# A two-layer GLA/FoX trunk on one core: key decay and output gate on GpSimd, a table root in two tasks, other modulation rates, more fills among the first sums, and the forget-gate product behind its weight tile

## The chip, the core and the metric

The kernel runs on one core of a Trainium2 chip. The engines it uses are TensorE (PE for its matmuls, PEld for its weight loads), VectorE (DVE), ScalarE (ACT), GpSimd (POOL) and SyncE (SP), which issues the DMAs. Each works through its own instructions in order, and they wait for one another by semaphores. The metric is the device time of one execution in microseconds, as the median of several. A change of less than 0.2% of it, 4.8 us, can't be told from none.

## The reference

A trunk of two layers on 256 tokens of width 2048, in fp32. Each layer is a token mixer and a gated MLP, and each of these is normalised, modulated by a conditioning vector `c`, and added back through a modulated gate:

```python
for i in range(2):
    sh_m, sc_m, g_m, sh_f, sc_f, g_f = split(c @ w_mod[i] + b_mod[i])
    h = rmsnorm(x, norm_mix[i]) * (1 + sc_m) + sh_m
    x = x + (1 + g_m) * mixer[i](h)            # 0: GLA, 1: FoX
    h = rmsnorm(x, norm_ffn[i]) * (1 + sc_f) + sh_f
    x = x + (1 + g_f) * conv_ffn(h)
```

The GLA mixer is a chunked gated linear attention with four heads. The change touches three places of it:

```python
q, k, v, r, a = split(h @ w_in)
b = cumsum(log_sigmoid(a @ w_gate + b_gate) / 16)       # in chunks of 64 tokens
k_inv = k * exp(-b);   k_end = k * exp(b_last - b)      # the key decay
o = attention(q * exp(b), k_inv, k_end, v)
o = rmsnorm(o, g_norm) * silu(r)                        # the root, the output gate
return o @ w_out
```

The FoX mixer is a causal softmax attention with a forget gate of 16 columns, `fl`, which come out of the same input product as q, k, v and the output gate: `q, k, v, og, fl = split(h @ w_in)`.

## The kernel before

Every weight matrix is streamed from HBM in tiles of 128 x 1024 fp32, loaded by SP into a ring of eight buffers (`RING`). A tile is split in two: ACT casts it to the reduced format of the matmul (`wh`, L140), and DVE subtracts that from the original (`wl`, L144). The activations are split in the same way, and three products are summed for each pair: high by high, high by low, low by high. So a weight tile costs PE 24 matmuls of 128x256 (L779, `stream_a`) or 12 of 128x512 (L860, `stream_b`). There are four buffers for split tiles, so ACT and DVE split up to three tiles ahead of the one PE works on (`AHEAD`).

`next_w` hands out the next tile and, on the way, issues the loads and splits of those ahead. Around every tile `tick()` runs other work: steps of the adaLN modulation, and tasks of a list `side`, both at a rate per tile held in `pace`. The order in which the program is written is then rearranged engine by engine by a scheduler, within what `tc.issue_after(x)` allows: what is written under it isn't placed ahead of instruction x.

**Modulations.** `c @ w_mod` is not done on PE: each 128-row piece of `w_mod` is multiplied by its element of c and added up on DVE (L289, L291, `acc`), 1.28 us for 128x1024, one piece in a step. When a sum is complete it rests for `REST` tiles, and is then turned by PE transposes (L322), added along the free axis on ACT (L326), and finished on DVE (L335, L344, L347). `BG0` and `BG1` are the rates of these steps in two stages of GLA, `N1` is the number of tiles over which the remaining steps are spread in the product behind GLA, and `LATE` the credit that this stage begins with.

**The start.** The first modulation, the shift of the first layer, is needed before anything else, and is computed on PE: pieces of `w_mod` by columns of c (L1517), a row copy on ACT (L1523), and eight one-column matmuls (L1526). Between these sums stand "fills" (L1563): matmuls on a constant that only keep PE busy, `KEEP` of them behind each sum. The first layer's normalised input `h` comes in blocks of 4, 5 and 7 tiles, since its modulation arrives in pieces, and the GLA input product runs over q, k, v0, v1, r0, r1 and a once for each block.

**GLA.** In the third block (`gla_rest`) the side tasks make the gate's cumulative sums, then the decayed queries (L1056 to L1062) and keys (`decay_k`, L1073 and L1074), the scores of the four heads (PE L1103, ACT L1108, DVE L1109 and L1110, mask on POOL L1112), their application to v (`apply`, PE L1125 and L1127, ACT L1131 and L1134), the sums of squares (DVE L1137 and L1138, PE L1141, DVE L1142 into `pvar`), their root (`table_root`: POOL L532, an ACT table function L533, and four refining operations on POOL, L534 to L537, into `grs`), the normalisation (`normalise`, with a broadcast by PE L445 and DVE L1153), and the output gate (`open_gate`: Silu on ACT L1168, product on DVE L1170). The result is split for the output product (ACT L682, DVE L683), which is `add_residual` with key `g_m`.

**FoX.** The v part of the input product runs over 16 row blocks in `stream_b`. From block 9 on (`GATE_AT`) `gate_part` adds the forget gate's product: it fetches a narrow weight tile of 128x368 (split into `nw`) and multiplies it with all h blocks so far, three matmuls of 128x256 each (L1231), then three more at each following block.

Of the kernel before, what the change touches and what calls it, by code (L numbers as in the profile page):

```python
# [18 lines left out]
P = 128  # L19
# [25 lines left out]
KEEP = 3  # L45
# [9 lines left out]
GP0 = 0.9  # L55
# [7 lines left out]
BG0, BG1 = 1.1, 1.1  # L63
N1, N2, N3, N4 = 22, 151, 150, 154
LATE = -3.0
# [15 lines left out]
def kernel(  # L81
# [184 lines left out]
    def mod_tasks(l, key, f0=0, fn=D, wide=False, defer=False, turn=False):  # L266
# [8 lines left out]
        def chunk(c0, kt, st):  # L275
# [5 lines left out]
            def f():  # L281
# [13 lines left out]
                elif last:  # L295
# [8 lines left out]
                    resting.append([REST, finish])  # L304
# [224 lines left out]
    def table_root(q, src, scale):  # L529
# [3 lines left out]
        nc.scalar.activation(q, v, AF.Abs_reciprocal_sqrt)  # L533
        nc.gpsimd.tensor_tensor(out=t, in0=v, in1=q, op=ALU.mult)  # L534
        nc.gpsimd.tensor_tensor(out=t, in0=t, in1=q, op=ALU.mult)
        nc.gpsimd.tensor_scalar(out=t, in0=t, scalar1=-0.5, scalar2=1.5, op0=ALU.mult, op1=ALU.add)
        nc.gpsimd.tensor_tensor(out=q, in0=t, in1=q, op=ALU.mult)  # L537
# [309 lines left out]
    def stream_b(kts, c0, lhs, base=None, extra=None):  # L847
# [4 lines left out]
        def mms(tt, k, wh, wl, lh, ll, n_=None):  # L852
            first, last = base is None and k == kts[0], k == kts[-1]
            ts_ = slice(tt * P, (tt + 1) * P)
            for hf in range(2):
                hs_ = slice(hf * 512, (hf + 1) * 512)
                o = ps[tt * 2 + hf]
                for i, (l_, w_) in enumerate(((lh, wh), (ll, wh), (lh, wl))):
                    if n_ is None or n_ == i:
                        mm = nc.tensor.matmul(o, l_[:, ts_], w_[:, hs_], start=first and i == 0, stop=last and i == 2,  # L860
                                              skip_group_check=True)
            return mm.ins
# [126 lines left out]
    def gla_rest(l, kts, pieces, piece, fold, parts):  # L989
# [80 lines left out]
        def decay_k(f0):  # L1070
            def f():
                fs = slice(f0, f0 + 4)
                nc.vector.tensor_tensor(out=kend[:, fs, :], in0=kinv[:, fs, :192], in1=ee[:, fs, :], op=ALU.mult)  # L1073
                nc.vector.tensor_tensor(out=kinv[:, fs, :], in0=kinv[:, fs, :], in1=enb[:, fs, :], op=ALU.mult)  # L1074
# [69 lines left out]

        def scale_of(hd):
            return lambda: table_root(grs[:, 2 * hd:2 * hd + 4], pvar[:, 2 * hd:2 * hd + 4], 1.0 / 512.0)
# [15 lines left out]
        side.extend((apply(2), apply(3), normalise(0), normalise(1), scale_of(2)))  # L1162
        pace["side"], pace["sacc"] = GP0, 0.0
        def open_gate(g, b):
            def f():
# [4 lines left out]
                nc.vector.tensor_tensor(out=o, in0=o, in1=th, op=ALU.mult)  # L1170
# [18 lines left out]
    def fox(l, h):  # L1189
# [32 lines left out]
        def gate_part(k):  # L1222
# [4 lines left out]
            for kk in range(0 if k == GATE_AT else k, k + 1):  # L1227
                gh, gl = h(kk)
                cs = slice(kk * FH, kk * FH + P)
                for i, (w_, r_) in enumerate(((gates["w"][0], gh), (gates["w"][0], gl), (gates["w"][1], gh))):  # L1230
                    nc.tensor.matmul(gates["p"][:, :T], w_[:, cs], r_, start=(kk == 0 and i == 0),  # L1231
                                     stop=(kk == KT - 1 and i == 2), skip_group_check=True)

# [287 lines left out]
    def early_finish(key, f0):  # L1521
# [3 lines left out]
        for m in range(HEAD):  # L1525
            nc.tensor.matmul(pt[:, m:m + 1], rows_[:, m * P:(m + 1) * P], one, start=(m == 0), stop=(m == HEAD - 1),  # L1526
                             skip_group_check=True)
# [22 lines left out]
    for i, args in enumerate(todo):  # L1550
# [8 lines left out]
        elif args[0] == "sh_m":  # L1559
            pw = psA.tile([P, 512], F32, tag="a", name=nm("pw"))  # L1560
            with tc.issue_after(summed):
                for _ in range(KEEP):
# [106 lines left out]
```

## Time and profile before

| | |
|---|---|
| median of 3 runs | 2410.9 us (2410.68 to 2413.03) |
| the profiled execution | 2411.13 us, of which the span is 2409.4 us |
| PE, PEld | busy 98% and 94% of the span |
| DVE, ACT, POOL | 78%, 56%, 2% |
| the chain that ended last | PE 92%, DVE 3%, DMA 3%, ACT 1%, issue 1% |
| HBM | 633 MB read, 264 GB/s over the span |

The profile is of one execution. A group of instructions has a line, an engine, an operation and names as `out<-in`; then come its count, its busy time, the mean of one, and the idle time of the engine just before its instructions, with what ended that idle time. In a timeline a row gives the start, the duration of a run of like instructions, and in brackets the idle time ahead of it. Matmuls overlap, so how far apart two of them start says more than their durations. PEclk is the share of full speed that TensorE was granted.

### The profile page before, as it was taken

The page shows a single profiled execution, that of the slowest core. Times are in us where ns is not written, and L with a number is a line of the kernel's source. Part 1 is how long each engine was busy: PE and PEld are TensorE (multiplying, and loading weights), DVE is VectorE, ACT ScalarE, POOL GpSimd, SP SyncE. Part 2 cuts the span into 40 slices and gives each one's busy share as a digit, 9 for nine tenths or more (in the row PEclk, how much of TensorE's full clock was granted, in tenths as well). Part 3 has the DMA queues.
Part 4 walks back from the last instruction along what each step waited for, and adds up shares of the span by engine and source line. Part 5 has one row for each costly group of instructions (what it writes and reads, how often), then busy time and mean ns, then how long its engine had stood idle before and what let it go on. Part 6 is the DMA issues. An engine that isn't in the chain of part 4 may idle for free.

```text
span 2409.4 us, 46946 instructions
## 1 busy us (share of the span) xinstructions
PE 2369.6 (98%) x19028; PEld 2274.7 (94%) x19030; DVE 1886.2 (78%) x2478; ACT 1347.1 (56%) x1932; POOL 45.6 (2%) x93
## 2 busy tenths in 40 slices
PE   7999999999999999999999999999999999999998
PEld 5899889999999999999888879999999999999998
DVE  5787979887679999986678888888777777777544
ACT  4668764645776566443554455545755555565433
POOL 0000000000000000000000201100000000000000
PEclk9999999999999999999999999999999999999999
DMA  9898869797669988998589877786777777766552
GB/s 375 326 353 297 312 229 325 275 361 273 199 200 310 314 310 311 324 315 301 158 297 314 303 267 236 241 296 234 227 236 237 228 235 236 235 206 216 192 191 101
DMA packets 188293, 638.31 MB, mean 265 GB/s; under 512 B 23849, under 2 KB 24859, under 8 KB 187692
## 3 DMA queue, kind: packets, MB, share of 16 engines
q1 hardware_dynamic: 187112, 634.12, 77.0%
q8 instruction: 149, 2.44, 0.4%
q10 hardware_dynamic: 964, 1.20, 0.1%
q14 instruction: 68, 0.56, 0.1%
HBM read 633.14 MB, written 2.10 MB: 264 GB/s over the span
## 4 chain that ended last, share of the span: by engine, by line
PE 92%; DVE 3%; DMA 3%; ACT 1%; issue 1%; DVEq 0%; SPq 0%; ACTq 0%
PE pa L779 74%; PE pa L860 14%; DMA wm<-in_w_mod_dram 1%; DVE wl L144 1%; DMA w<-in_fox_w_in_dram 0%; DVE acc L291 0%; DMA w<-in_gla_w_in_dram 0%; DVE hn L623 0%; PE pm L1103 0%; PE pm L1330 0%; PE pm L1276 0%; PE pm L1294 0%; ACT wh L140 0%; PE pm L1293 0%; PE pm L1125 0%
## 5 line engine op out<-in xcount | busy, mean ns | idle before, releaser
L140 ACT CAST wh<-w 128x1024 fp32r<-128x1024 f32 x816 | 852.1, 1049 | 903.2 <-PE pa L779 651.4
L144 DVE TENSOR_TENSOR wl<-w,wh 128x1024 fp32r<-128x1024 f32 x816 | 991.7, 1218 | 405.4 <-ACT wh L140 399.3
L779 PE MATMUL pa<-h,wh 128*128 128x256 f32 x7168 | 1223.5, 278 | 5.0 <-DVE h L653 3.6
L779 PEld LDWEIGHTS pa<-h,wh 128*128 128x128 f32 x7168 | 1073.9, 188 | 10.5 <-DVE h L653 4.2
L779 PE MATMUL pa<-h,wl 128*128 128x256 f32 x3584 | 966.3, 277 | 1.9 <-DVE wl L144 1.9
L779 PEld LDWEIGHTS pa<-h,wl 128*128 128x128 f32 x3584 | 662.5, 188 | 2.7 <-DVE wl L144 2.5
L779 PE MATMUL pa<-op,wh 128*128 128x256 f32 x3840 | 651.6, 277 | 0.4 <-DVE op L683 0.2
L779 PEld LDWEIGHTS pa<-op,wh 128*128 128x128 f32 x3840 | 573.0, 188 | 1.4 <-DVE xT L912 1.0
L779 PE MATMUL pa<-op,wl 128*128 128x256 f32 x1920 | 518.0, 276 | 0.0
L291 DVE SCALAR_TENSOR_TENSOR acc<-wm,cT,acc 128x1024 f32<-128x1024 f32 (+2 forms) x360 | 444.4, 1235 | 15.1 <-DMA wm<-in_w_mod_dram 13.9
L779 PEld LDWEIGHTS pa<-op,wl 128*128 128x128 f32 x1920 | 355.0, 188 | 0.0
L860 PE MATMUL pa<-wh,h 128*128 128x512 f32 x1024 | 312.0, 394 | 0.2 <-ACT h L644 0.2
L860 PEld LDWEIGHTS pa<-wh,h 128*128 128x128 f32 x1024 | 191.1, 188 | 40.3 <-ACT h L644 0.9
L860 PE MATMUL pa<-wl,h 128*128 128x512 f32 x512 | 191.8, 394 | 0.0
L860 PEld LDWEIGHTS pa<-wl,h 128*128 128x128 f32 x512 | 96.5, 189 | 19.5
L1382 ACT ACTIVATE y<-u,cw 128x256 f32<-128x256 f32 x176 | 101.7, 599 | 3.3 <-DVE act L1398 1.3
L1385 DVE SCALAR_TENSOR_TENSOR y<-u,cw,y 128x254 f32<-128x254 f32 x176 | 83.3, 479 | 2.9
L1383 DVE SCALAR_TENSOR_TENSOR y<-u,cw,y 128x255 f32<-128x255 f32 x176 | 84.0, 477 | 0.0
L1404 ACT COPY u<-pa 128x512 f32<-128x512 f32 x112 | 63.6, 582 | 2.1 <-PE pa L779 1.2
L644 ACT ACTIVATE h<-hn,mod 128x256 fp32r<-128x256 f32 x58 | 32.4, 596 | 14.0 <-DVE hn L623 11.3
L1392 ACT ACTIVATE u<-y 128x256 f32<-128x256 f32 x88 | 36.0, 413 | 3.3 <-DVE y L1385 3.1
L1398 DVE TENSOR_TENSOR act<-u,y 128x256 f32<-128x256 f32 x88 | 36.7, 420 | 1.4
(274 smaller groups left out, 1044.5 us busy)
## 6 DMA issues: line engine op xcount, KB each, us to landing
wm<-in_w_mod_dram SPq DMA_DIRECT2D x320, 512.0 KB, 5.3
w<-in_ffn_w_up_dram SPq DMA_DIRECT2D x320, 512.0 KB, 4.5
w<-in_ffn_w_down_dram SPq DMA_DIRECT2D x176, 512.0 KB, 4.6
w<-in_fox_w_in_dram SPq DMA_DIRECT2D x128, 512.0 KB, 5.2
w<-in_gla_w_in_dram SPq DMA_DIRECT2D x96, 512.0 KB, 7.1
w<-in_gla_w_out_dram SPq DMA_DIRECT2D x32, 512.0 KB, 5.9
w<-in_ffn_w_up_dram SPq DMA_DIRECT2D x64, 256.0 KB, 4.0
w<-in_fox_w_out_dram SPq DMA_DIRECT2D x32, 512.0 KB, 5.1
```

Of the source, the lines that this page charges most:

```text
L140: order["b"], order["c"] = order["c"], nc.scalar.copy(out=hi, in_=src).ins
L144: order["v"] = nc.vector.tensor_tensor(out=lo, in0=src, in1=hi.bitcast(F32), op=ALU.subtract).ins
L291: nc.vector.scalar_tensor_tensor(out=st["a"], in0=wt[:, j, :], scalar=col, in1=st["a"], op0=ALU.mult, op1=ALU.add)
L644: hot = nc.scalar.activation(hi, t, AF.Identity, scale=sc, bias=sh).ins
L779: mm = nc.tensor.matmul(o, w_[:, ms], r_, start=(first and i == 0 and m % 2 == 0), stop=last and i == 2, skip_group_check=True)
L860: mm = nc.tensor.matmul(o, l_[:, ts_], w_[:, hs_], start=first and i == 0, stop=last and i == 2, skip_group_check=True)
L1382: nc.scalar.activation(y, u, AF.Identity, scale=cw[:, l * 3 + 2, r:r + 1], bias=cw[:, 6 + l, r:r + 1])
L1383: nc.vector.scalar_tensor_tensor(out=y[:, 1:], in0=u[:, :T - 1], scalar=cw[:, l * 3 + 1, r:r + 1], in1=y[:, 1:], op0=ALU.mult, op1=ALU.add)
L1385: nc.vector.scalar_tensor_tensor(out=y[:, 2:], in0=u[:, :T - 2], scalar=cw[:, l * 3, r:r + 1], in1=y[:, 2:], op0=ALU.mult, op1=ALU.add)
L1392: nc.scalar.activation(u, y, AF.Silu)
L1398: nc.vector.tensor_tensor(out=act[m // 8][:, m % 8, :], in0=sg, in1=y, op=ALU.mult)
L1404: nc.scalar.copy(out=u[:, 2 * b:2 * b + 2, :], in_=ps[b])
```

## The change

It has seven parts:

- **Fills.** `KEEP` becomes a number for each of the four sums of the first shift: 3, 11, 4, 4 instead of 3, 3, 3 and none. The last four come behind the one-column matmuls.
- **Rates.** `BG0` 1.1 to 0.95, `BG1` 1.1 to 1.0, `N1` 22 to 24, `LATE` -3 to -2, and `GP0`, the rate of the side tasks in one stage, 0.9 to 1.1.
- **Rest.** The modulations of the first layer's `h`, those that are loaded wide and turned by PE, rest one tile instead of two.
- **Root.** `table_root` does only its first operation; what follows comes back as a task of its own (`root_of`), with the ACT function ordered behind the latest weight cast. The side list then runs apply(2), root_of(0), apply(3), scale_of(2), normalise(0), normalise(1), root_of(2).
- **Key decay.** The four products of `decay_k` go from DVE to POOL.
- **Output gate.** The eight products of `open_gate` go from DVE to POOL.
- **Narrow product.** At block 9 `gate_part` only fetches its weights; the products of blocks 0 to 10 are made at block 10, ordered behind the last matmul written by then.

```diff
-KEEP = 3
+KEEP = (3, 11, 4, 4)
-GP0 = 0.9
+GP0 = 1.1
-BG0, BG1 = 1.1, 1.1
-N1, N2, N3, N4 = 22, 151, 150, 154
-LATE = -3.0
+BG0, BG1 = 0.95, 1.0
+N1, N2, N3, N4 = 24, 151, 150, 154
+LATE = -2.0
...
-                    resting.append([REST, finish])
+                    resting.append([1 if turn and wide else REST, finish])
...
         nc.gpsimd.tensor_scalar(out=v, in0=src, scalar1=scale, scalar2=EPS, op0=ALU.mult, op1=ALU.add)
-        nc.scalar.activation(q, v, AF.Abs_reciprocal_sqrt)
...
+
+        def rest():
+            with tc.issue_after(order["c"]):
+                nc.scalar.activation(q, v, AF.Abs_reciprocal_sqrt)
...
+        return rest
...
+            order["mm"] = mm.ins
             return mm.ins
...
-                nc.vector.tensor_tensor(out=kend[:, fs, :], in0=kinv[:, fs, :192], in1=ee[:, fs, :], op=ALU.mult)
-                nc.vector.tensor_tensor(out=kinv[:, fs, :], in0=kinv[:, fs, :], in1=enb[:, fs, :], op=ALU.mult)
+                nc.gpsimd.tensor_tensor(out=kend[:, fs, :], in0=kinv[:, fs, :192], in1=ee[:, fs, :], op=ALU.mult)
+                nc.gpsimd.tensor_tensor(out=kinv[:, fs, :], in0=kinv[:, fs, :], in1=enb[:, fs, :], op=ALU.mult)
...
-        side.extend((apply(2), apply(3), normalise(0), normalise(1), scale_of(2)))
+        side.extend((apply(2), root_of(0), apply(3), scale_of(2), normalise(0), normalise(1), root_of(2)))
...
-                nc.vector.tensor_tensor(out=o, in0=o, in1=th, op=ALU.mult)
+                nc.gpsimd.tensor_tensor(out=o, in0=o, in1=th, op=ALU.mult)
...
             if k == GATE_AT:
                 gates["w"], gates["p"] = next_w(0, [(4 * D, FH)]), misc()
-            for kk in range(0 if k == GATE_AT else k, k + 1):
+                return
+            es = gates["es"] = ExitStack()
+            es.enter_context(tc.issue_after(order["mm"]))
+            for kk in range(0 if k == GATE_AT + 1 else k, k + 1):
...
+            es.close()
...
-            nc.tensor.matmul(pt[:, m:m + 1], rows_[:, m * P:(m + 1) * P], one, start=(m == 0), stop=(m == HEAD - 1),
-                             skip_group_check=True)
+            order["o"] = nc.tensor.matmul(pt[:, m:m + 1], rows_[:, m * P:(m + 1) * P], one, start=(m == 0),
+                                          stop=(m == HEAD - 1), skip_group_check=True).ins
...
         if args[2] == 3:
             early_finish(*args[:2])
-        elif args[0] == "sh_m":
-            pw = psA.tile([P, 512], F32, tag="a", name=nm("pw"))
+        if args[0] == "sh_m":
+            if i < len(todo) - 1:
+                pw = psA.tile([P, 512], F32, tag="a", name=nm("pw"))
+            else:
+                summed = order["o"]
             with tc.issue_after(summed):
-                for _ in range(KEEP):
+                for _ in range(KEEP[args[2]]):
                     nc.tensor.matmul(pw, fill[:, :P], fill, start=True, stop=True)
```

The scheduler and the pools decide what this does to the order on an engine. Three places are shown; line numbers of the changed kernel are a few higher, and the numbers behind the names differ between the two kernels.

**PE in the v stream of FoX.** A name `pa` is one of the stream's four sums, `wh` and `wl` are the parts of a weight tile, `nw` those of the narrow one. Before:

```order
L860 MATMUL pa_14385<-wh_14509,h_14454 128x512
L1231 MATMUL pm_14644<-h_14347,nw_14584 128x256 x2
L860 MATMUL pa_14382<-wh_14509,h_14454 128x512
L860 MATMUL pa_14382<-wl_14510,h_14454 128x512
L860 MATMUL pa_14383<-wh_14509,h_14454 128x512
L860 MATMUL pa_14383<-wl_14510,h_14454 128x512
L860 MATMUL pa_14384<-wh_14509,h_14454 128x512
L860 MATMUL pa_14384<-wl_14510,h_14454 128x512
L860 MATMUL pa_14385<-wh_14509,h_14454 128x512
L860 MATMUL pa_14385<-wl_14510,h_14454 128x512
L860 MATMUL pa_14382<-wh_14534,h_14552 128x512
```

And of the change, where `wh_14573` is the tile that was `wh_14560`:

```order
L864 MATMUL pa_14398<-wh_14573,h_14565 128x512
L864 MATMUL pa_14398<-wl_14574,h_14565 128x512
L1246 MATMUL pm_14657<-h_14360,nw_14597 128x256 x12
L1246 MATMUL pm_14657<-h_14467,nw_14597 128x256 x12
L1246 MATMUL pm_14657<-h_14565,nw_14597 128x256 x9
L864 MATMUL pa_14395<-wh_14622,h_14565 128x512 x2
L864 MATMUL pa_14395<-wl_14623,h_14565 128x512
```

Two narrow matmuls stood in the midst of the tile `wh_14509`, and the others in and behind the next one. Now they stand together, behind the rest of that tile (8 matmuls), the whole of the next and the whole of the one after. On ACT nothing moves here: the cast of `nw` stands ahead of that of `wh_14534` (now `wh_14547`) in both kernels.

**PE ahead of the second block of h.** The transposes L322 turn the modulation that the second block waits for. Before:

```order
L779 MATMUL pa_982<-h_310,wh_988 128x256 x2
L779 MATMUL pa_983<-h_310,wh_988 128x256 x2
L779 MATMUL pa_984<-h_310,wh_988 128x256 x2
L322 MATMUL pm_1049<-ident,acc_735 128x128 x4
L322 MATMUL pm_1058<-ident,acc_735 128x128
L779 MATMUL pa_981<-h_310,wh_944 128x256 x2
L779 MATMUL pa_981<-h_310,wl_945 128x256
```

And of the change, where `wh_923`, `wh_957` and `wh_1001` are the block's last three tiles:

```order
L783 MATMUL pa_997<-h_323,wh_1001 128x256 x2
L322 MATMUL pm_1032<-ident,acc_748 128x128 x4
L322 MATMUL pm_1041<-ident,acc_748 128x128
L783 MATMUL pa_994<-h_323,wh_923 128x256 x2
L783 MATMUL pa_994<-h_323,wl_924 128x256
L783 MATMUL pa_994<-h_323,wh_923 128x256 x2
L783 MATMUL pa_994<-h_323,wl_924 128x256
L783 MATMUL pa_994<-h_323,wh_957 128x256 x2
```

The six products with `wh_923` and `wl_924` now stand behind the transposes. Between these and the end of the block there were 24 matmuls of 128x256 and the 12 of the narrow product `a`; there are 30 and 12. Behind the third block's modulation there were 41 matmuls of the block, and there are 66.

**ACT at the end of GLA.** The names are `gsq`, the squares; `th`, the output gate; `grs`, the root; `op`, the split operand of the output product. Before:

```order
L1134 ACTIVATE oT_2796<-pm_3466,vec 128x256 x2
L326 ACTIVATE pm_3514,red_3513<-pm_3514 128x128
L533 ACTIVATE grs<-rv_3617 128x4
L326 ACTIVATE pm_3514,red_3513<-pm_3514 128x128
L326 ACTIVATE pm_3523,red_3513<-pm_3523 128x128
L326 ACTIVATE pm_3514,red_3513<-pm_3514 128x128
L326 ACTIVATE pm_3523,red_3513<-pm_3523 128x128
L326 ACTIVATE pm_3514,red_3513<-pm_3514 128x128
L326 ACTIVATE pm_3523,red_3513<-pm_3523 128x128
L140 CAST wh_3586<-w_3330 128x1024
```

And of the change:

```order
L1139 ACTIVATE oT_2803<-pm_3463,vec 128x256 x2
L1180 ACT_TABLE_LOAD
L1180 ACTIVATE th_3677<-r_169_989 128x512
L1180 ACTIVATE th_3737<-r_169_989 128x512
L1180 ACTIVATE th_3773<-r_169_989 128x512
L1180 ACTIVATE th_3809<-r_169_989 128x512
L536 ACT_TABLE_LOAD
L536 ACTIVATE grs<-rv_3511 128x4
L326 ACTIVATE pm_3656,red_3655<-pm_3656 128x128 x3
L686 CAST op_3894<-oT_2802 128x512
L326 ACTIVATE pm_3656,red_3655<-pm_3656 128x128
L686 CAST op_3894<-oT_2802 128x512
```

Behind the last of these rows come one more L326 and then the cast of the next weight tile, `wh_3682`. Before, no weight was cast between the first root and the place shown; now two casts stand there. The gate's table load, its four functions, the second root with a table load of its own, and two operand casts that wait for POOL's gate products stand ahead of the next one.

More of the change, by code (lines that the diff above doesn't have):

```diff
@@ L532, in table_root @@
         nc.gpsimd.tensor_scalar(out=v, in0=src, scalar1=scale, scalar2=EPS, op0=ALU.mult, op1=ALU.add)
-        nc.scalar.activation(q, v, AF.Abs_reciprocal_sqrt)
[L534 to L537, printed above, removed]
+        def rest():
+            with tc.issue_after(order["c"]):
+                nc.scalar.activation(q, v, AF.Abs_reciprocal_sqrt)
+            nc.gpsimd.tensor_tensor(out=t, in0=v, in1=q, op=ALU.mult)
+            nc.gpsimd.tensor_tensor(out=t, in0=t, in1=q, op=ALU.mult)
+            nc.gpsimd.tensor_scalar(out=t, in0=t, scalar1=-0.5, scalar2=1.5, op0=ALU.mult, op1=ALU.add)
+            nc.gpsimd.tensor_tensor(out=q, in0=t, in1=q, op=ALU.mult)
+        return rest
     def token_rstd(q, n_):
@@ L1143, in apply, with f, root_of @@
             return f
+        roots = {}
         def scale_of(hd):
-            return lambda: table_root(grs[:, 2 * hd:2 * hd + 4], pvar[:, 2 * hd:2 * hd + 4], 1.0 / 512.0)
+            def f():
+                roots[hd] = table_root(grs[:, 2 * hd:2 * hd + 4], pvar[:, 2 * hd:2 * hd + 4], 1.0 / 512.0)
+            return f
+        def root_of(hd):
+            return lambda: roots.pop(hd)()
         def normalise(hd):
```

## The prediction

> **What bounds the kernel now.** First the page's busy times, then the waits of PE, then a table of stretches: busy time of each engine with its instruction count, the clock granted to PE, the busy share of the DMA engines and GB/s.
>
> ```profile
> PE 2369.6 (98%) x19028; PEld 2274.7 (94%) x19030; DVE 1886.2 (78%) x2478; ACT 1347.1 (56%) x1932; POOL 45.6 (2%) x93
> ...
> L140 ACT CAST wh<-w 128x1024 fp32r<-128x1024 f32 x816 | 852.1, 1049 | 903.2 <-PE pa L779 651.4
> ```
>
> ```profile
> PE pa L779 <- DVE h L653: 3.6, 3, 2.9
> ...
> PE pm L1141 <- DVE gsq L1138: 2.9, 2, 2.0
> PE pm L1231 <- ACT nw L140: 2.5, 1, 2.5
> ```
>
> ```profile
> 24.00:36.00 12.00, 7.27 (x49) 2.33 (x42) 1.08 (x5) 1.90 (x3) 0.23 (x2) 0.96 1.04 395
> 36.00:42.00 6.00, 5.72 (x27) 5.72 (x28) 5.70 (x10) 4.54 (x7) 0.00 (x0) 0.51 1.04 401
> 42.00:107.00 65.00, 65.00 (x477) 61.10 (x476) 53.81 (x67) 37.21 (x67) 0.00 (x0) 1.00 0.99 385
> 107.00:112.00 5.00, 2.12 (x12) 1.92 (x11) 4.70 (x9) 5.00 (x9) 0.00 (x0) 0.81 0.72 252
> ...
> 242.00:322.00 80.00, 78.40 (x592) 70.29 (x591) 70.35 (x85) 54.96 (x101) 6.34 (x15) 1.00 0.88 314
> 322.00:340.00 18.00, 13.51 (x102) 12.34 (x101) 8.13 (x14) 12.67 (x36) 0.98 (x5) 1.00 0.16 50
> ...
> 1190.00:1204.00 14.00, 11.47 (x47) 9.16 (x46) 7.71 (x15) 7.40 (x13) 0.00 (x0) 0.88 0.66 168
> ```
>
> PE is the bound. ACT's casts wait 651 us for PE to free a buffer, so the splits run ahead, and what DVE or ACT does more cheaply is worth nothing by itself: only PE's idle time can be won, and the time in which its clock is halved. The change removes no matmul and adds twelve fills. What it can reach are the places above: the start (4.7 us idle before 36, then six us at half clock), the stop at 107, the hole of 18 − 13.5 = 4.5 us at 322 to 340, the stop at 1196.
>
> **The start.** A timeline of PE:
>
> ```profile
> 29.75 1.07 PE L1517 MATMUL pe<-wm,cz 128*32 128x512 f32 x8 [1.95 <-DMA wm<-in_w_mod_dram]
> ...
> 32.46 1.06 PE L1517 MATMUL pe<-wm,cz 128*32 128x512 f32 x8 [0.89 <-DMA wm<-in_w_mod_dram]
> 34.23 1.16 PE L1526 MATMUL pm<-ones,er 128*128 128x1 f32 x8 [0.71 <-ACT er L1523]
> 36.28 2.08 PE L779 MATMUL pa<-h,wh 128*128 128x256 f32 x8 [0.89 <-ACT h L644]
> ```
>
> Eleven fills, by the 0.82 us of three in a row about 0.27 each, take 3.0 us instead of 0.8 and cover the 1.95 us wait for `wm`; one more covers little. PE still waits for the same data, so these cost nothing at most places. What they can change is the clock: 0.96 over 12 us is 0.5 us lost, so half speed began about 35, and 0.51 over the next 6 says that it lasted to about 41.9. In that time PE did 2.8 us worth of products from 36.28 on. The idle time just before 35 (0.89 and 0.71) isn't touched, so I take it that the clock still falls; the four fills then take 0.5 us each at half speed, fill the 0.89 us wait and push the first product to about 37.2 (**+0.9** if nothing else happens). If in return the clock is back after half of the time, at about 38.5, the work done by 41.9 is 0.6 + 3.4 = 4.0 instead of 2.8. I take **−1.3**, from −2.8 (no fall) to +0.9. Weights allow it: they arrive at a DMA share of 0.99, but PE had no idle time in 42 to 107.
>
> The Trainium skill ("TensorE: Matmul & The Clock Gate", What's actually happening) says that the clock follows PE's activity in free-running windows of 3413 ns. The 6.8 us here are two such windows, which agrees. By it one full window is won back, 1.7 us of work, less what the fills push away; and where the window lies differs between executions.
>
> **The rest of one tile.** The stop at 107, in timelines of DVE and PE:
>
> ```profile
> 96.03 2.72 DVE L291 SCALAR_TENSOR_TENSOR acc<-wm,cT,acc 128x640 f32<-128x640 f32 x3
> ...
> 101.63 0.85 PE L779 MATMUL pa<-h,wh 128*128 128x256 f32 x6
> 102.32 0.71 PE L322 MATMUL pm<-ident,acc 128*128 128x128 f32 x5
> ...
> 110.62 1.22 PE L779 MATMUL pa<-h,wh 128*128 128x256 f32 x4 [2.88 <-DVE h L653]
> ...
> 184.69 0.39 PE L779 MATMUL pa<-h,wl 128*128 128x256 f32 x1 [0.64 <-DVE wl L144]
> ```
>
> The sum is ready at 98.75, its transposes run at 102.32, and the second block's h comes 8.3 us later. Six matmuls of (102.32 − 101.63) / 6 = 0.115 us now stand behind the transposes: 0.7 us. On DVE a weight split has also changed places with the copy behind the narrow product, which waited: 0.3. So **−1.0** of the 2.9. The sum is early enough by 3.6 us for this and the start's gain together. Half speed again: 0.81 over five us is 1.9 us at half clock, up to 112 and beyond, where the next 71 us have some more of it (their clock is 0.99); if it is half as long as at the start, 3.4 us, it cost 1.7 us of work. With a stop of 1.9 us it may or may not come; **−0.9**, from 0 to −1.7. At 184 PE waited 0.64 for a weight split behind the next block's chain, whose transposes now come 25 matmuls, 2.9 us, earlier: **−0.6**, from 0.
>
> **The narrow product.** ACT, DVE and PE around 1198:
>
> ```profile
> 1190.18 1.03 ACT L140 CAST wh<-w 128x1024 fp32r<-128x1024 f32 x1
> ...
> 1198.82 0.50 ACT L140 CAST nw<-w 128x368 fp32r<-128x368 f32 x1 [6.60 <-DMA w<-in_fox_w_in_dram]
> 1199.22 1.04 ACT L140 CAST wh<-w 128x1024 fp32r<-128x1024 f32 x1
> ```
>
> ```profile
> 1200.29 1.23 DVE L144 TENSOR_TENSOR wl<-w,wh 128x1024 fp32r<-128x1024 f32 x1 [0.40 <-DMA w<-in_fox_w_in_dram]
> ```
>
> ```profile
> 1195.77 1.07 PE L860 MATMUL pa<-wh,h 128*128 128x512 f32 x4
> 1199.37 0.80 PE L1231 MATMUL pm<-h,nw 128*128 128x256 f32 x2 [2.53 <-ACT nw L140]
> ...
> 1206.03 1.22 PE L1231 MATMUL pm<-h,nw 128*128 128x256 f32 x9
> ```
>
> PE waits for `nw`, which waits for its load, and then runs at half speed for a while (PEclk 0.88 over 14 us: 3.4 us at half). The wait doesn't go: ACT still casts `nw` first, and the next weight tile's `wh` only at 1199.22, done at 1200.26. Without the narrow matmuls PE has 8 of 12 matmuls left of the tile at hand. At 0.23 us each (1195.77 to 1196.68 are four) they last from 1196.7 to 1198.5. Then **PE waits for that cast**, 1.75 us, which is late next. From 1200.26 the twelve of this tile take 2.75 and perhaps 0.3 for `wl` (1201.5): 1203.3. Before, the same work was done at 1206.03, with 5 narrow matmuls, 0.6 us, in it. So 1206.0 − 0.6 − 1203.3 = 2.1: **−2.1**. It includes the clock: a stop of 1.75 us is shorter than those of 2.9 and 2.5 behind which it fell. If it falls all the same, −0.6; if the load comes earlier, −4.
>
> **POOL for DVE.** Four products leave DVE at the key decay, eight at the gate. What POOL does in a row of that size the trace doesn't show; the nearest are the masks L1112, one beside a busy DVE and one beside an idle one:
>
> ```profile
> 286.51 1.28 DVE L291 SCALAR_TENSOR_TENSOR acc<-wm,cT,acc 128x1024 f32<-128x1024 f32 x1
> ...
> 289.56 1.42 DVE L144 TENSOR_TENSOR wl<-w,wh 128x1024 fp32r<-128x1024 f32 x1
> ```
>
> ```profile
> 286.63 1.42 POOL L1112 TENSOR_SCALAR_AFFINE_SELECT at<-at 128x256 f32<-128x256 f32 x1 [36.55 <-DVE at L1110]
> ...
> 319.50 0.41 POOL L1112 TENSOR_SCALAR_AFFINE_SELECT at<-at 128x256 f32<-128x256 f32 x1 [1.17 <-DVE at L1110]
> ```
>
> ```profile
> 261.27 0.65 ACT L1033 ACTIVATE ee<-ee 128x384 f32<-128x384 f32 x1
> ```
>
> ```profile
> 272.58 1.82 DVE L1073 TENSOR_TENSOR kend<-k,ee 128x768 f32<-128x768 f32 x2
> ...
> 276.65 2.36 DVE L1074 TENSOR_TENSOR k<-k,enb 128x1024 f32<-128x1024 f32 x2
> ```
>
> ```profile
> L1103 PE MATMUL pm<-q,kend x96: 221/222/223, 280.7 to 317.8; 128*64 128x64 f32 x96
> ```
>
> With d for a product of 128x512, the free mask gives 0.8 us and the hindered one 2.9 (1.42 x 2). Two inputs speak for more than 0.8; I take **1.1**, nearer the free one, since the mask waited for a running DVE instruction just once. The key decay is 7d in all, 7.7 us. Its inputs are there at 261.9 (L1033), PE needs it at 280.7: 18.8 us. It is hidden, and DVE's 4.2 us less are too, since ACT and DVE are ahead: **0**, from 0 to +1.5 at d = 2.9 (20.3 us).
>
> **The hole and the root.** PE and ACT before:
>
> ```profile
> 330.12 0.58 PE L1141 MATMUL pm<-ones,gsq 128*128 128x1 f32 x4 [1.96 <-DVE gsq L1138]
> ```
>
> ```profile
> 328.68 0.83 ACT L1134 ACTIVATE oT<-pm,vec 128x256 f32<-128x256 f32 x2
> ...
> 339.51 1.28 ACT L1168 ACT_TABLE_LOAD   x1
> 340.81 2.20 ACT L1168 ACTIVATE th<-r 128x512 f32<-128x512 f32 x4
> ```
>
> The waits for `gsq` (2.9) go, since products of later tiles stand ahead of L1141 now. But counted from the end of the last `apply`, ACT has an estimated 1.5 us until its last copies are done (0.83, the squares ahead of them), a table load of 1.28, four functions of 2.2, another load and the root 1.5: 6.5. POOL refines in 1.2 and makes the two gate products in 2.2, to 9.9; behind their operand casts the weight cast ends at about **12**. PE's work ahead of that tile (53 products of 0.115, and an estimated 3 for transposes, broadcasts and a wait among them) lasts to about 9. So PE stops for 3, and for 1 to 1.5 more at its `wl` and at L445: as much as the 4.5 that go. In one piece it is long enough for the clock to fall, 1.7 us, which I count half: **+0.8**, from −1.5 to +1.7. The rates move modulation steps from one stage to the next on a DVE that isn't the bound: 0.
>
> **Sum.** −1.3 − 1.0 − 0.9 − 0.6 − 2.1 + 0 + 0.8 = −5.1. From the profiled execution's 2411.1 (its span and 1.7 us around it) that is 2406.0. The median is 0.2 below that execution: **2405.8**.
>
> **Rivals.**
> - *The clock stays up, and the hole closes to 3 us.* Start −2.6, 107 −2.7, 184 −0.6, narrow −2.1, hole −1.5: −9.5, 2401.4. For it: the idle times shrink at all places. Against it: two remain at 1.8 to 1.9 us.
> - *What is won at the start is lost again*, so the change doesn't do what it says there: the fills hold up the first product, or the second block's h comes when its data does, at a DMA share of 0.99. Left are −1.0 at 107, −2.1 at the narrow product, and the hole with its clock +1.7: −1.4, 2409.5.
> - *POOL and DVE hinder each other*, and PE ends up behind both. At d = 2.9 the key decay holds POOL for 20.3 us beside a DVE that is idle for a quarter of 9.65 us in such a stretch (80 − 70.35). If DVE stands still for that time, it gains 4.2 and 2.4 and falls behind by 13.7; the three tiles ahead, 72 x 0.115 = 8.3 us, leave 5.4 for PE. The key decay is 1.5 late as well, and behind each half's first two gate products the cast comes 2 x 1.8 later, twice: 7.2. So +14.1: 2419.9. For it speaks the row at 289.56, a split of 1.42 beside the mask, where the mean is 1.22. It becomes slower than before by 0.2% from d of about 2.6.
>
> The Trainium skill ("SBUF — State Buffer", SBUF: two separate sides) gives the rule behind this rival: a DVE operation with two SBUF inputs and a GpSimd operation that reads SBUF share a port pair as an exclusive lock, and the later one waits for the whole instruction. The rows agree: the mask at 286.63 ended 0.26 us after DVE's at 287.79.
>
> **Chances.** Forecast 0.43, clock and hole 0.24, lost start 0.22, POOL 0.11. A difference under 4.8 us can't be measured, and the forecast lies at that edge, at 2406.1: two thirds of it count as faster. Faster 0.29 + 0.24 = 0.53, same 0.14 + 0.21 = 0.35, slower 0.11 + 0.01 = 0.12. The range 2399 to 2413 leaves out POOL and the lower end of the second case. For the forecast by itself it is 2403.5 to 2408.
>
> **What would show it.** PEclk in 36 to 42 near 0.75 or more; the stop at 107 at 1.9; a wait of L860 for ACT's `wh` of 1.5 to 2 where L1231 waited 2.5; the key decay's products on POOL under 2.5 us each; one stop of about 3 us in the output product's first tiles, for a `wh` that stands behind operand casts on ACT. It would be wrong if POOL's products take over twice my 1.1, or if the second root blocks ACT for much longer than those 6.5 us.

## The result, and the profile after

The changed kernel takes **2422.8 us** (median of 6 runs, 2420.6 to 2427.2) beside 2410.8 before: 1.005 times as long, 95% interval 1.0038 to 1.0063. The forecast was 2405.8 in a range of 2399 to 2413. The mechanism of the rival in which POOL and DVE hinder each other shows in the trace, and its 2419.9 lies 2.9 us below the result; but it is only a part of the cause. The other part is the rates, which the prediction counted as 0.

The page and PE's waits after:

```profile
PE 2374.6 (98%) x19043; PEld 2275.9 (94%) x19043; DVE 1889.6 (78%) x2466; ACT 1349.6 (56%) x1934; POOL 72.4 (3%) x105
```

```profile
PE pm L462 <- DMA xtok<-in_x_dram: 6.1, 2, 4.2
PE pm L322 <- DVE acc L291: 4.7, 1, 4.7
PE pa L783 <- DVE wl L144: 3.8, 4, 1.2
PE pa L783 <- DVE h L657: 2.8, 4, 1.9
...
PE pm L322 <- DVE oT L1165: 2.0, 2, 1.3
PE pm L1108 <- POOL k L1079: 1.9, 1, 1.9
PE pa L783 <- DVE op L687: 1.7, 1, 1.7
PE pa L864 <- ACT wh L140: 1.7, 1, 1.7
PE pm L1146 <- DVE gsq L1143: 1.6, 1, 1.6
```

The first row, the wait for the input at the start, is as before (5.9). The greatest of the others is one that before hardly had (0.4 us): PE's transposes L322 for a modulation's sum. The table of stretches, with the columns of before:

```profile
36.00:42.00 6.00, 5.76 (x35) 4.67 (x33) 5.24 (x11) 4.92 (x7) 0.23 (x2) 0.77 1.04 399
107.00:112.00 5.00, 3.14 (x21) 2.93 (x20) 4.93 (x11) 5.00 (x10) 0.00 (x0) 0.84 0.78 286
242.00:322.00 80.00, 75.83 (x568) 67.41 (x568) 70.93 (x76) 54.83 (x99) 16.49 (x17) 1.00 0.80 274
322.00:340.00 18.00, 17.99 (x146) 17.44 (x144) 8.26 (x16) 12.96 (x24) 1.06 (x4) 1.00 0.61 215
340.00:395.00 55.00, 48.59 (x412) 47.32 (x412) 49.91 (x50) 32.50 (x55) 16.56 (x12) 1.00 0.70 243
395.00:452.00 57.00, 51.38 (x430) 50.98 (x429) 46.52 (x50) 25.82 (x54) 0.00 (x0) 0.94 0.98 354
```

The clock came back sooner at the start (0.77 instead of 0.51), PE worked through 3.1 instead of 2.1 us of the stop at 107, and the hole at 322 to 340 is closed. But PE lost 2.6 us more than before in 242 to 322, stood idle for 6.4 in 340 to 395, and for 5.6, with some half clock, in 395 to 452. In before the second of these stretches was full:

```profile
340.00:395.00 55.00, 54.48 (x476) 54.10 (x476) 51.69 (x58) 32.88 (x55) 0.00 (x0) 1.00 0.88 304
```

Since all kernels make the same 18048 weight products (L779 and L860), I compare the time at which the n-th of them starts, as kernel less before, in us (counted from the traces; one profiled execution each):

| kernel | 540th | 1140th | 1680th | 2160th | 3000th | last | median us | before beside it |
|---|---|---|---|---|---|---|---|---|
| the change | −1.2 | −0.2 | +3.2 | +5.4 | +13.3 | +12.6 | 2422.8 | 2410.8 |
| gate_dve | −3.3 | −1.2 | +3.2 | +1.1 | +9.8 | +10.6 | 2420.1 | 2409.7 |
| decay_dve | −3.4 | −1.6 | −2.1 | −0.1 | +7.9 | +8.4 | 2418.7 | 2409.7 |
| both_dve | −3.3 | −0.8 | −1.7 | −3.1 | +5.2 | +4.9 | 2415.8 | 2409.7 |
| rates_old | −3.4 | −1.8 | +2.8 | +6.3 | +7.5 | +6.8 | 2419.2 | 2409.7 |
| pool_only | −1.8 | −1.2 | +4.4 | +7.1 | +8.7 | +8.2 | 2420.6 | 2411.1 |
| rates_only | +0.3 | +1.3 | +1.2 | −1.9 | +9.8 | +10.4 | 2420.4 | 2411.1 |
| kept | −1.9 | +0.3 | −0.2 | +1.4 | +0.8 | 0.0 | 2412.2 | 2411.1 |
| kept_rest2 | −0.8 | −0.9 | −0.9 | −0.7 | −1.1 | −1.3 | 2409.8 | 2410.9 |
| rest_only | −0.9 | +0.3 | −0.1 | +1.5 | +1.3 | +2.2 | 2413.3 | 2409.7 |
| narrow_only | −1.8 | −2.5 | −2.5 | −2.4 | −2.8 | −4.3 | 2409.8 | 2411.1 |
| fills_narrow | −1.2 | −1.0 | −0.9 | −0.6 | −0.9 | −2.7 | 2410.4 | 2410.9 |
| bg_only | −1.7 | −1.8 | −1.9 | −4.9 | +3.3 | +0.7 | 2414.6 | 2410.9 |
| n1_only | −1.3 | +0.1 | +0.6 | +1.6 | +2.2 | +2.2 | 2410.6 | 2410.9 |

The 540th is behind the stop at 107, the 1140th at 205, the 1680th before the end of GLA's scores, the 2160th in the middle of the output product, the 3000th behind it. Up to the 540th chance has a part of some 2 us, by where half clock falls: bg_only, n1_only and narrow_only have the start of before and lead there too.

### The profile page after: what moved, and what is told of

It reads as the page before. It is cut to its first block, busy times and chain, and to the rows that moved or that the text cites. A ratio compares the mean times of both kernels' runs of the same rounds, so it can differ in the third digit from the quotient of the medians.

```text
span 2422.0 us, 46969 instructions
## 1 busy us (share of the span) xinstructions
PE 2374.6 (98%) x19043; PEld 2275.9 (94%) x19043; DVE 1889.6 (78%) x2466; ACT 1349.6 (56%) x1934; POOL 72.4 (3%) x105
## 4 chain that ended last, share of the span: by engine, by line
PE 87%; DVE 5%; DMA 4%; ACT 2%; issue 2%; POOL 0%; DVEq 0%; SPq 0%; ACTq 0%; POOLq 0%
PE pa L783 72%; PE pa L864 11%; DMA wm<-in_w_mod_dram 2%; DVE wl L144 2%; DMA w<-in_gla_w_in_dram 1%; DVE acc L291 1%; ACT wh L140 1%; DMA w<-in_fox_w_in_dram 0%; DVE hn L627 0%; PE pm L1346 0%; PE pm L1292 0%; PE pm L1310 0%; DMA w<-in_gla_w_out_dram 0%; PE pm L1309 0%; ACT pa L765 0%
## 5 line engine op out<-in xcount | busy, mean ns | idle before, releaser
L144 DVE TENSOR_TENSOR wl<-w,wh 128x1024 fp32r<-128x1024 f32 x816 | 993.9, 1221 | 412.8 <-ACT wh L140 407.0
L783 PE MATMUL pa<-op,wl 128*128 128x256 f32 x1920 | 523.7, 277 | 2.1 <-DVE wl L144 2.1
L291 DVE SCALAR_TENSOR_TENSOR acc<-wm,cT,acc 128x1024 f32<-128x1024 f32 (+2 forms) x360 | 448.1, 1245 | 19.2 <-DMA wm<-in_w_mod_dram 17.8
L917 DVE SCALAR_TENSOR_TENSOR xT<-pa,mod,xT 128x256 f32<-128x256 f32 x64 | 28.7, 478 | 13.3 <-PE pa L783 12.9
L434 POOL TENSOR_TENSOR rt<-rv,qrs 128x16 f32<-128x16 f32 x12 | 7.1, 591 | 1036.4 <-DVE qrs L431 1035.7
```

The costliest lines, as they stand in the source:

```text
L144: order["v"] = nc.vector.tensor_tensor(out=lo, in0=src, in1=hi.bitcast(F32), op=ALU.subtract).ins
L291: nc.vector.scalar_tensor_tensor(out=st["a"], in0=wt[:, j, :], scalar=col, in1=st["a"], op0=ALU.mult, op1=ALU.add)
L783: mm = nc.tensor.matmul(o, w_[:, ms], r_, start=(first and i == 0 and m % 2 == 0), stop=last and i == 2, skip_group_check=True)
L917: nc.vector.scalar_tensor_tensor(out=xT[:, m, :], in0=ps[pair][:, j, :], scalar=modcol(l, key, m), in1=xT[:, m, :], op0=ALU.mult, op1=ALU.add)
```

## The experiments

**Which move loses it?** Four kernels undo one part each.

```diff
# gate_dve: the change with
+                nc.vector.tensor_tensor(out=o, in0=o, in1=th, op=ALU.mult)
# decay_dve: the change with
+                nc.vector.tensor_tensor(out=kend[:, fs, :], ...)
+                nc.vector.tensor_tensor(out=kinv[:, fs, :], ...)
# both_dve: both of these
# rates_old: the change with
+BG0, BG1 = 1.1, 1.1
+N1, N2, N3, N4 = 22, 151, 150, 154
+LATE = -3.0
```

> The change with the eight products of the output gate back on DVE; all else as changed. POOL theory (the gate's products on POOL, 2.0 us each in the changed kernel against 0.68 on DVE, hold ACT's operand casts and DVE): the loss between the end of GLA and the middle of the output product goes (some 4 us), and DVE, relieved of four stretched instructions of 1.05 us, finishes the sum that PE waited 4.7 us for at 442 in time or nearly so: 2410 to 2413. Rates theory (the modulation steps moved later are what makes that sum late): the wait at 442 stays at 4 to 5 us with its half clock behind it, and only the 4 us ahead of it go: 2418 to 2419.

> The change with the four products of the key decay back on DVE. POOL theory: PE's wait of 1.9 us for the decayed key at 279 goes, and DVE gains what four of its instructions were stretched by, 7.5 us, less the 4.2 us that come back; the waits behind the gate stay: 2418 to 2420. Rates theory: the same 2 us, 2420 to 2421, with the wait at 442 unchanged. A sum that becomes ready at 442 with this alone would speak for DVE's lag since 272 as its cause: 2411 to 2413.

> The change with the four numbers of the modulation pace (BG0, BG1, N1, LATE) as before. Rates theory: the steps come earlier, the wait for the sum at 442 goes with its half clock: 8 us, 2413 to 2415. POOL theory: the steps only stand earlier in a queue of DVE that has no room for them between 272 and 380, so stops of PE for weight splits there take the place of the wait: 2419 to 2424.

> The change with both moves to POOL undone (key decay and output gate on DVE). POOL theory: what is left is the gain of the fills, the rest of one tile and the narrow product, some 2 us in the changed kernel's first 200 us and at 1200: 2407 to 2410. Rates theory: the wait at 442 stays, 2416 to 2418.

Neither theory has it alone: 2420.1, 2418.7, 2419.2 and 2415.8. The second and third lie in the POOL theory's ranges, the fourth 0.2 below that of the rates, and the first above both. In the table, the key decay on POOL loses about 5 us up to the 1680th product (−2.1 and −1.7 without it, +2.8 to +3.2 with it), and the gate on POOL some 3 to 4 up to the 2160th (from +1.1 to +5.4, from −3.1 to −0.1). With the old rates nothing is lost behind the 2160th but 1.2; with the new ones 8, with POOL (+5.4 to +13.3) and without it (−3.1 to +5.2). Ahead of the 2160th the new rates win: `kept`, which is `both_dve` with the old ones, stands at +1.4 there.

**The parts alone.** Before, with only the new rates, or only the moves to POOL (`nc.gpsimd` in L1073, L1074 and L1170):

> The kernel before with the four numbers of the modulation pace alone (BG0 0.95, BG1 1.0, N1 24, LATE -2). Rates theory (the numbers alone leave the modulation's sum behind the place where PE wants its transposes): a wait of L322 for the sum of 4 to 5 us in 380 to 450, with half a clock window or two behind it, 6 to 8 us: 2416 to 2418 beside a before of about 2410. POOL theory (the sum is late because DVE lost time to POOL): the steps fit, 2409 to 2412.

> The kernel before with the key decay and the output gate on POOL, and nothing else. POOL theory: DVE instructions beside POOL's are stretched to 1.3 to 2.9 us, PE waits for the decayed key and behind ACT's operand casts: 5 us at the key decay and 3 to 4 at the gate, 2417 to 2420. If the costs were only in the new order of the side tasks (the root as a task): 2410 to 2412.

Both costs are there, 2.4 and 0.6 above the ranges given: 2420.4, which is 1.0037 (1.0024 to 1.0050) of before, and 2420.6, 1.0041 (1.0027 to 1.0056). Added to before, each alone costs nearly as much as the whole change (+10.4 and +8.2 in the table, together +12.6). Beside the rest of the change they do add up, nearly: from `kept` (0.0), which has neither, the rates take it to +4.9 (`both_dve`), POOL to +6.8 (`rates_old`) and both to +12.6; the ratios to before are 1.0008, 1.0026, 1.0038 and 1.0050. Why the rates cost more in before than beside the rest isn't shown.

**How POOL costs it.** POOL and then DVE in the changed kernel, at the key decay and at the gate:

```profile
272.83 5.62 POOL L1078 TENSOR_TENSOR kend<-k,ee 128x768 f32<-128x768 f32 x2 [21.01 <-DVE q L1067]
278.42 5.64 POOL L1079 TENSOR_TENSOR k<-k,enb 128x1024 f32<-128x1024 f32 x2
...
343.33 5.01 POOL L1182 TENSOR_TENSOR oT<-oT,th 128x512 f32<-128x512 f32 x4
363.11 6.92 POOL L1182 TENSOR_TENSOR oT<-oT,th 128x512 f32<-128x512 f32 x2 [14.77 <-DVE oT L1165]
```

```profile
273.86 2.87 DVE L144 TENSOR_TENSOR wl<-w,wh 128x1024 fp32r<-128x1024 f32 x1
276.66 2.88 DVE L291 SCALAR_TENSOR_TENSOR acc<-wm,cT,acc 128x1024 f32<-128x1024 f32 x1
279.46 2.31 DVE L335 TENSOR_TENSOR mod<-red,bm 128x8 f32<-128x8 f32 x1
281.80 2.28 DVE L347 TENSOR_SCALAR mod<-mod 128x8 f32<-128x8 f32 x1
...
363.08 1.28 DVE L291 SCALAR_TENSOR_TENSOR acc<-wm,cT,acc 128x1024 f32<-128x1024 f32 x1
364.28 2.35 DVE L144 TENSOR_TENSOR wl<-w,wh 128x1024 fp32r<-128x1024 f32 x2
366.55 2.32 DVE L291 SCALAR_TENSOR_TENSOR acc<-wm,cT,acc 128x1024 f32<-128x1024 f32 x1
368.79 1.78 DVE L687 TENSOR_TENSOR op<-oT,op 128x512 fp32r<-128x512 f32 x1
```

At 343 DVE has nothing to do, and a product of 128x512 takes POOL 1.25. At 363, beside DVE, two take 6.9. The two engines hold each other up: an operation of 128x8, 0.16 us by itself, takes 2.31 beside a product of 128x1024, which is 2.1 more; the split L144 takes 1.65 more beside one of 128x768; L291 1.05 more beside a gate product. So d, POOL's own time, is 1.05 to 1.25, as I took it. What was wrong is that I let it run beside DVE. DVE is rid of 4.2 us of key decay and stands still for 1.65 + 1.6 + 2.15 + 2.1 = 7.5, and POOL's product waits in turn. They don't always go one by one: at 363 POOL's first product takes 4.7, since three DVE instructions go ahead of it at their usual lengths. The rule of the Trainium skill ("SBUF — State Buffer", SBUF: two separate sides), an exclusive lock for the whole instruction, agrees with each of the stretched rows.

Nor did POOL begin at 261.9, where the inputs are ready in before (265.4 in the change), but at 272.8, behind DVE's L1067: DVE's last product with the queries. So PE waits 1.9 us for `k`. At the gate ACT waits instead:

```profile
ACT op L686 <- POOL oT L1182: 9.2, 6, 4.2
ACT wh L140 <- DMA w<-in_gla_w_out_dram: 3.0, 1, 3.0
```

Nine microseconds of ACT's time go to operand casts that wait for POOL, with weight casts queued behind them.

**Why the rates lose it.** First, which pair of numbers:

```diff
# bg_only: before with
+BG0, BG1 = 0.95, 1.0
# n1_only: before with
+N1, N2, N3, N4 = 24, 151, 150, 154
+LATE = -2.0
```

> The kernel before with BG0 0.95 and BG1 1.0 alone. If fewer steps ahead of the output product are what makes its modulation late, and the pace in the product (set from what is left, over 22 tiles) doesn't make up for it: one or two waits of L322 for acc, 3 to 6 us: 2413 to 2417. If the pace makes up for it, since it is worked out from the steps that remain: 2410 to 2412.

> The kernel before with N1 24 and LATE -2 alone. If the slower pace in the output product is the cause: the waits of L322 at the end of its two halves, 3 to 6 us, 2413 to 2417. If the two pairs only cost together (less done before, and a slower pace after), each alone stays within 2 us of before.

BG alone is 2414.6, 1.0019 (1.0010 to 1.0029); N1 and LATE alone change nothing, 0.9998 (0.9989 to 1.0007); together they cost about twice as much as BG. With BG, 38 steps of the modulation instead of 42 lie between the 960th and the 1800th product, and 10 and 20 instead of 13 and 13 in the next two lots of 420. In bg_only the hole at the end of GLA is gone and PE leads by 4.9 us at the 2160th; all of it, and more, is lost by the 3000th (+3.3), at two waits of L322 (3.7 together), one for `xT` (1.7) and in 3.4 us of half clock. So it is the lower `BG` that closes the hole: in all ten kernels that have it PE no longer waits for `gsq` at 322 to 340, and in all nine with the old one it waits 2.7 to 3.9 us, also in `kept` and `kept_rest2`, which have the new order of the root. The row of `kept`:

```profile
PE pm L1146 <- DVE gsq L1143: 3.9, 2, 2.0
```

For bg_only I took it that the pace was too slow to catch up, and made it faster:

```diff
# bg_n19: bg_only with N1 = 19
# bg_n17_narrow: bg_only with N1 = 17, and the narrow product of the change
```

> The kernel before with BG0 0.95, BG1 1.0 and N1 19. Deadline theory (the lower rates leave more steps to the output product, whose pace from N1 sets when they are done; the sums miss PE's transposes at the ends of its halves only by that): a faster pace takes the waits of L322 (3.7 us with BG alone, and the half clock behind the second) away, and the closed hole at 323 to 340 stays won: 2405 to 2408 beside a before of about 2410.5. Rival (DVE has no room for the steps there, whatever the pace): the waits turn into ones for weight splits, 2411 to 2415.

> The kernel before with BG0 0.95, BG1 1.0, N1 17 and the narrow product behind its tile. Deadline theory: as with N1 19, with a step or two more in hand, and 1.4 us from the narrow product: 2404 to 2407. Rival (no room on DVE): 2410 to 2415, the more the faster the pace.

The deadline theory falls: 2418.6 and 2421.8, the faster the worse. The rival falls as well: both lie above its 2411 to 2415, and PE waits for sums, not for weight splits (0.3 us in bg_n19). The waits of PE for such a sum, first in bg_n17_narrow, then in bg_late5_narrow, which follows below and has N1 22:

```profile
PE pm L322 <- DVE acc L291: 12.2, 2, 7.3
```

```profile
PE pm L322 <- DVE acc L291: 5.2, 1, 5.2
```

When does DVE finish the four sums that it makes between 205 and 437 (two halves of `g_m`, and the first halves of the FFN's scale and shift)? The end of the last L291 of the fourth, where its transposes stand (the number of weight products ahead of them), and when they ran:

| kernel | fourth sum ends | transposes behind product | they start |
|---|---|---|---|
| before | 434.7 | 2610 | 435.9 |
| bg_n17_narrow | 435.8 | 2520 | 435.8 |
| bg_n19 | 437.0 | 2568 | 437.1 |
| bg_only | 435.7 | 2604 | 435.8 |
| bg_late5_narrow | 436.8 | 2616 | 436.8 |
| rates_only | 441.8 | 2610 | 441.9 |
| pool_only | 440.2 | 2610 | 442.6 |
| the change | 446.7 | 2610 | 446.8 |

With the lower `BG` the fourth sum ends at 435 to 437 whatever the pace between 17 and 22 (with 24, in rates_only, at 441.8). A faster pace doesn't finish it earlier, it only puts its transposes further ahead in PE's order, and PE then stops with work behind them. The third sum does end earlier, at 394.7, 395.6 and 398.6 for 17, 19 and 22, but for 17 and 19 its transposes stand 78 and 54 products further ahead than for 22, 9.0 and 6.2 us of PE's work, and PE waits 7.3, 4.5 and 1.1 us for it. In before, DVE was busy for 216 of the 234 us from the 1100th product to the end of the fourth sum, and the loads run at a DMA share of 0.98 and more from 390 on; DVE is the third busy time in these rows:

```profile
340.00:365.00 25.00, 24.85 (x218) 24.64 (x217) 25.00 (x31) 19.22 (x27) 0.00 (x0) 1.00 0.85 288
365.00:390.00 25.00, 24.64 (x218) 24.47 (x217) 22.95 (x24) 8.70 (x12) 0.00 (x0) 1.00 0.89 305
390.00:415.00 25.00, 25.00 (x222) 24.99 (x221) 23.74 (x29) 15.86 (x32) 0.00 (x0) 1.00 0.98 349
415.00:440.00 25.00, 25.00 (x223) 25.00 (x222) 21.53 (x20) 11.72 (x25) 0.00 (x0) 1.00 1.02 382
```

In before, PE arrives 1.2 us after the sum. So I take **DVE's chain of sums as a second bound, as long as PE's work to within about a microsecond.** By it, closing the hole only brings PE to the sum sooner. This is inferred from where the sums end: no run made DVE's part shorter, and none separates DVE's own work from the loads that it waits for. POOL's cost doesn't need this wait: in pool_only and rates_old, with the old rates, PE comes to the fourth sum 2.4 and 3.0 us after its end, and 7.1 and 6.3 us are lost already at the 2160th product.

A later place was the test of this:

```diff
# bg_late5_narrow: bg_only with LATE = -5, and the narrow product of the change
# bg_n26_narrow: bg_only with N1 = 26, and the narrow product of the change
```

> The kernel before with BG0 0.95, BG1 1.0, N1 22 and LATE -5, and the narrow product behind its tile. Place theory (DVE and the DMA queues finish the steps when they can, whatever the pace; the pace only sets where PE's transposes stand in PE's own order, and PE stops there): the transposes stand 26 and 12 products later than with LATE -3, so the two waits of 1.1 and 2.6 shrink to 0 and about 1.2, the half clock behind the second goes, and with 1.4 us from the narrow product it is 2407 to 2410 beside 2410.5. If the steps simply come later by as much: waits as with BG alone, 2412 to 2415.

> The kernel before with BG0 0.95, BG1 1.0, N1 26 and LATE -3, and the narrow product behind its tile. Place theory: the transposes stand 30 and 84 products later than with N1 22, the second ones at the very end of the output product, so neither waits for the sum; but the residual behind the second half then waits for them, 2 to 3 us: 2409 to 2412. If the slower pace itself makes the sums late: 2414 or more.

Little of it holds. With LATE −5 the first wait goes, but the second is 5.2 instead of 2.6, since PE arrives at it earlier and the sum doesn't end sooner: 2414.6, not the 2407 to 2410 that I gave it. With N1 26 no transpose waits for a sum any more, as forecast; they come at 447, behind the whole product, and the residual waits for them, 3.2 us for ACT's sums of L326 and 2.7 for L522, with 10.2 us of half clock: 2416.2, not 2409 to 2412. Both times fit the other theory's ranges, and with N1 26 the fourth sum does end later, at 442.5. I found no pace with which the lower rates win.

**The rest of the change.**

```diff
# kept: the change without POOL and with the old rates
# kept_rest2: kept with
+                    resting.append([REST, finish])
# rest_only: before with
+                    resting.append([1 if turn and wide else REST, finish])
# narrow_only: before with the change of gate_part and order["mm"]
# fills_narrow: narrow_only with the change of KEEP and of the loop around it
```

> The change without its moves to POOL and without its rates: fills, rest of one tile, root as a task, GP0 and narrow product. If POOL and the rates are all that it loses by: the start and the stop at 107 give 3.3 us, the third block takes 1.5 to 2.5 of it back, the root and the narrow product give 1 to 2: 2406 to 2408 beside a before of about 2410. If the root's new order costs by itself: 2409 to 2412.

> The change without POOL, without its rates, and with the rest of two tiles as before: fills, root as a task, GP0, narrow product. If the rest of one tile is what loses 2.9 us between 135 and 190 in the same kernel with it: the milestone at 190 stays at the lead that the start and the stop at 107 leave, and the time is 2 us lower than with it, 2408 to 2411. If the fills or chance in the clock window set that lead: the same within 1 us.

> The kernel before with the rest of one tile alone. If it wins 1 us at the second block and loses 1.5 to 3 at the third: 2410.5 to 2412.5 beside 2410.5, with a stop of 1.9 at 107 and a wait for wl of 1.2 at 184. If the loss in the other kernel came from its fills or the clock: 2409 to 2410.

> The kernel before with the narrow product behind its tile, and nothing else. By my prediction PE's wait for nw (2.5 us) becomes one for the next cast of wh of 1.7 us, and 2.1 us are won: 2407.5 to 2408.5 beside a before of 2410. If the wait for wh is followed by others, for the h blocks that the narrow product's position moved, less than 1: 2409 to 2410.

> The kernel before with the fills and the narrow product alone. By the parts measured so far (start 0.4 to 1.1, narrow 1.4) 2408 to 2409.5 beside a before of about 2410.5; with the stop at 107 untouched, its half clock comes or not by where the window lies.

`kept` is 1.0008 (0.9999 to 1.0016), `kept_rest2` 0.9999 (0.9990 to 1.0008), `rest_only` 1.0014 (1.0005 to 1.0022), `narrow_only` 0.9995 (0.9986 to 1.0004), `fills_narrow` 1.0001 (0.9992 to 1.0010). Of the five, `kept` (2412.2), `rest_only` (2413.3) and `fills_narrow` (2410.4) lie above the ranges that I gave first, and `narrow_only` (2409.8) has less than the 2.1 us of the prediction. So the rest of one tile costs: with it (`kept`) the lead of 1.9 us at the 540th product is gone at the 1140th, without it (`kept_rest2`) the lead of 0.8 stays. It does win some 0.8 us at the second block (kept −1.1 to −1.9 from the 480th to the 540th, kept_rest2 −1.1 to −0.8), and loses 1.0 to 2.6 from there to the 1140th in the seven kernels that have it (the others lie between 0.7 won and 1.4 lost), at the third block, where PE waits 1.2 for `wl` at 183. Why that split comes later there I did not settle. The root and the order of its side tasks cost or win nothing that can be told (kept_rest2 and fills_narrow are alike within 0.6 us). In the narrow product's place PE now waits for `wh`, as forecast; ACT and then PE in the changed kernel:

```profile
1212.14 0.50 ACT L140 CAST nw<-w 128x368 fp32r<-128x368 f32 x1 [6.64 <-DMA w<-in_fox_w_in_dram]
1212.54 1.04 ACT L140 CAST wh<-w 128x1024 fp32r<-128x1024 f32 x1
```

```profile
1213.64 1.21 PE L864 MATMUL pa<-wh,h 128*128 128x512 f32 x4 [1.70 <-ACT wh L140]
1215.58 0.50 PE L864 MATMUL pa<-wh,h 128*128 128x512 f32 x1 [0.73 <-DVE h L657]
```

Behind that wait of 1.7 (forecast 1.75) comes a second one of 0.7 for the next block's h. Over this place (the 9000th to the 9600th product) the change wins 0.7 and `narrow_only` 1.4, not 2.1, though neither has half clock there and before has 3.4 us of it. Sorted by half clock the new place wins nothing that can be told: the five profiles that have the narrow product behind its tile and half clock there lie between 0.7 lost and 0.3 won, five with the old place between 1.0 lost and 0.4 won; without half clock seven win 0.6 to 1.9, and bg_only, with the old place, 2.5. But half clock stays away in seven of twelve with the new place, and in one of seven with the old one. No version beat before by more than its interval; `narrow_only` is the nearest to it.

## Why the prediction was wrong, point by point

- **Rates: "0", "on a DVE that isn't the bound".** This step failed. Alone they cost 9.4 us, 1.0037 (1.0024 to 1.0050). The lower `BG` closes the hole (bg_only −4.9 at the 2160th product), and behind it PE loses more than that (rates_only from −1.9 to +9.8) at transposes that wait for DVE's sums. In before the fourth sum ends at 434.7 and PE arrives at 435.9, a slack of 1.2 us, which the mean (DVE 78%) hides. That DVE is the bound there is inferred, as said above.
- **Key decay: "0, from 0 to +1.5", "it is hidden".** This failed too: about +5 up to the 1680th product. The size d = 1.1 was right for POOL's own time (1.05 to 1.25); that it lies beside DVE's was wrong, and so was the start at 261.9. With the waiting, a product took 2.35 to 3.33 us at the key decay and 1.74 to 4.68 at the second half of the gate.
- **Gate and hole: +0.8.** The hole closed as said (PE 17.99 of 18 us), but by the rates, not by the root. What took its place behind it was 6.4 us of idle PE in 340 to 395, not 4 to 4.5, and in other pieces: not one stop of about 3 for `wh` (0.9), but waits for `oT` (2.0), `op` (1.7) and `wl` (1.7). POOL's products beside DVE were counted at 1.1 instead of 1.7 to 4.7.
- **Start −1.3.** The change has 13 fills more (22 for 9), not the twelve counted. The half clock did shorten as said: of eight profiles with the fills five have 3.4 us of it at the start and three none, of eleven without them ten have 6.8. At the 480th product the eight lead by 1.0 to 1.2, the change by 0.4; those without stand at +0.2 to −0.7, but n1_only at −1.4. So the gain was smaller than −1.3, and no time shows it (fills_narrow 1.0001).
- **Second block −1.0 and −0.9.** The six matmuls moved ahead give some 0.8. The half clock behind the stop stays away in four of the seven profiles with the rest of one tile and in five of twelve without it: chance has a large part in it. With start and second block together, the −3.2 of the sum was −3.3 or −3.4 in four of the six kernels that have both edits, −1.9 in kept and −1.2 in the change.
- **Third block −0.6:** wrong in sign, +1.0 to +2.6.
- **Narrow product −2.1:** −0.7 in the change and −1.4 in narrow_only, and as far as the profiles tell by half clock only. The wait that takes its place was right to 0.05 us in the change; what I left out is the wait for h behind it.
- **The POOL rival, 2419.9,** had the place right. That its total lies near the result is luck: it counts 14.1 us for POOL, on top of a forecast gain of 5.1, and nothing for the rates. The runs show 7 to 9.5 for POOL, next to none of the gain (kept 1.0008), and 5 to 10 for the rates. I gave it 0.11, since I took one stretched split (1.42 for 1.22) as the size of the effect, and it was the remainder of a mask that DVE had held up.

## What to carry to other kernels

Before an elementwise product goes from VectorE to GpSimd, look at what VectorE runs at that time: in this kernel the times of such a pair added up (a split of 1.22 us took 2.87 beside a product of 128x768, which had taken VectorE 0.95), so that by this sum VectorE is relieved only by products that are shorter on GpSimd. A share of busy time says nothing about a deadline: follow each slow side chain to the instruction that needs its end, and compare the two arrival times, here 434.7 and 435.9. If the end doesn't move with the pace, a faster pace only moves the consumer forward in an in-order queue, and makes it worse.

## What the runs showed that was not expected

A VectorE instruction of 128x8, 0.16 us by itself, took 2.31 us beside a GpSimd product of 128x1024. Half clock came in pieces of 3.4 us or a multiple of it in all runs, but for the last piece, which the end of the program cuts: around the wait of 4.7 us at 442 there were 6.8 us of it, and from the 2600th to the 2700th product the change lost 7.2. Kernels that have the start of before lie 1.9 us ahead of it to 0.3 behind it at the 540th product, by where these pieces fall; the fills were to win 1.3.
